# A list scheduler's picture of waits, products of constants in TensorE's gaps, and chunk values copied out by two engines, in a two-layer RWKV-7 and latent-attention trunk

## The chip, the cores and the metric

The kernel runs on one NeuronCore of a Trainium2 chip. Its five instruction streams are TensorE (PE; its weight loads are shown apart as PEld), VectorE (DVE), ScalarE (ACT), GpSimd (POOL) and SyncE (SP), which starts the DMAs. The metric is the device time of one execution in microseconds (us); the smaller is the better.

## The reference, cut to what matters

The input is a sequence of 512 positions with 16 learned ones put ahead, so T = 528, of width 1024. Layer 0 projects it (w_in, 2048 wide per kind) to v, k, r and a gate g and to two small products for decay and a, and then runs a recurrence over time, independently for 32 heads of 64 channels:

```python
def step(S, inp):
    r_t, w_t, k_t, v_t, a_t, b_t = inp
    sa = jnp.einsum('bhij,bhj->bhi', S, a_t)
    S = S * w_t[:, :, None, :] + sa[..., None] * b_t[:, :, None, :] + v_t[..., None] * k_t[:, :, None, :]
    return S, jnp.einsum('bhij,bhj->bhi', S, r_t)
```

The result is normalised per head, gated and projected by w_out. Layer 1 is a causal attention with 16 heads over low-rank keys and values, gated and projected again. All is float32 at the interface.

## The kernel before

Layer 0 keeps channels on partitions and time on the free axis. Two heads share a tile (a pair p = 0 to 15; head 0 on partitions 0 to 63, head 1 on 64 to 127). The recurrence is done in chunks: chunk 0 holds the 16 learned positions, chunks 1 to 8 hold 64 positions each. For a pair, `products` and `inverse` make the triangular matrices of all nine chunks (many small products, half of them float16), and `chunk(p, ci)` then runs the nine steps one after the other. A step goes: two products into PSUM (`ALR` by `SV`), VectorE copies them to `xs`, two products (`xs` by `Qf`), ScalarE copies the two halves into `SV`, two products (`SV` by `KBt`), VectorE scales and adds the two halves into `SV` of the next chunk with `sd`, which GpSimd made ready. The next chunk waits for that. Chunks 1 to 7 are run by `recur`, which takes its PSUM from the pool `pc` of one bank; chunks 0 and 8 are run by `ends` and take it from the pool `pw` of four banks. That is 7 x 16 = 112 steps on `pc` and 32 on `pw`.

Between these steps TensorE does the projections of k, r and g (`gemm`, `multiply`): each output is 48 products of 128x264, two PSUM banks at a time. A number is split into a high and a low float32r part, so every product is done three times (high by high, high by low, low by high). Layer 1 works in the same way with larger products.

Nothing of this order is written by hand. Every part is a generator (a stage) that yields steps; `Flow.note` records the instructions of a step in place of issuing them, and `Flow.run` is a list scheduler. For each stage's first open step `Flow.start` works out when each of its operations could begin: when its engine is free (`self.free`), when its inputs are ready plus a lag from engine to engine (`LAGS`), and when the PSUM bank it touches was last used by another engine (`self.access`). The operation with the earliest start is issued, and `Flow.issue` moves the picture on by the operation's cost (`Flow.cost`). The line that chooses is

```python
if s[1][j].wide and self.hungry(t):
    t -= self.AHEAD
if best is None or t < best[0] - (self.SLACK if i > best[1] else -self.SLACK):
    best = (t, i, j)
```

Stages stand in order of rank: finish, recur, ends, sides, invert, within, prepare and so on, the layer-1 stages, the weights' loads and splits, and the large products (`gemm`, `gating`) last. With SLACK at zero the earlier start wins whatever the rank. `wide` marks an operation of TensorE with 256 columns or more; where the scheduler's own count of columns says that TensorE is short of work (`hungry`), a wide product is taken 0.25 us early. The engines carry out what they are given in that order, each waiting for its semaphores; a picture that is wrong about a wait costs time on the engine that reaches the waiting instruction. All instructions are issued by one line (293 before the change, 306 after), so the trace's groups are told apart by the names of their tiles.

## Time and profile before

| what | value |
|---|---|
| median of 3 runs | 1622.15 us (1618.94 to 1629.05) |
| the profiled execution's own time | 1630.59 us |
| its span, from the first to the last instruction | 1628.6 us |
| mean granted TensorE clock, as a share of 2.4 GHz | 0.954 |
| busy TensorE / VectorE / ScalarE / GpSimd | 92% / 62% / 59% / 50% of the span |
| TensorE products (and as many weight loads) | 13788 |

A stretch is named by its start and end in us from the span's start. Layer 0's recurrence runs from about 246 to 960 us, its last large products to 1107, layer 1 behind that. A busy time counts an instruction from its start to its end; products of TensorE overlap, so 100% busy is not its peak. The granted clock is 1.00 (2.4 GHz) or 0.50 (1.2 GHz) at any one moment.

### The profile page before, as it was taken

The numbers are of one execution on the slowest core, as the hardware profiler recorded it, in microseconds if no ns is written. First come the engines' busy times: TensorE is split into PE (matmuls) and PEld (weight loads), VectorE is DVE, ScalarE is ACT, GpSimd is POOL, SyncE is SP. The second block draws the span as 40 slices with busy tenths as digits, with TensorE's granted clock in tenths as the row PEclk, the third lists the DMA queues.
The fourth block names the chain that finished last, engine by engine and source line by source line (L and its number), as shares of the span: only waits on it lengthen the run. The fifth ranks groups of instructions, "written<-read, shape, count | busy, mean of one in ns | idle before, by whom it ended". The sixth has DMA issues, their size and how long they took to land. (4 is left out here: it accounts for less than half of the span.)

```text
span 1628.6 us, 36087 instructions
## 1 busy us (share of the span) xinstructions
PE 1498.6 (92%) x13788; PEld 1292.3 (79%) x13788; DVE 1006.9 (62%) x2144; ACT 967.1 (59%) x2451; POOL 806.3 (50%) x1039
## 2 busy tenths in 40 slices
PE   4889889999999999998899999999989999999997
PEld 3889878777877877777787889998778888877786
DVE  7994677788778678777664542035366666666503
ACT  3557657876767677775686865445454544544532
POOL 5353566566556465554565565745522222332554
PEclk8999999999989899998897999999989999999999
DMA  3446522122112121121402247532211111111332
GB/s 112 143 173 230 188 85 87 41 68 74 68 58 71 42 77 65 61 81 55 167 35 73 86 139 256 159 110 92 68 52 40 56 46 52 59 56 43 110 93 82
DMA packets 84700, 148.66 MB, mean 91 GB/s; under 512 B 9392, under 2 KB 18480, under 8 KB 84528
## 3 DMA queue, kind: packets, MB, share of 16 engines
q1 hardware_dynamic: 84528, 146.37, 27.7%
q8 instruction: 108, 1.77, 0.4%
q14 instruction: 64, 0.52, 0.1%
HBM read 112.87 MB, written 33.46 MB: 90 GB/s over the span
## 5 line engine op out<-in xcount | busy, mean ns | idle before, releaser
L293 POOL TENSOR_TENSOR w<-wraw,w 128x512 fp32r<-128x512 f32 (+1 forms) x278 | 358.7, 1296 | 431.3 <-ACT w L293 393.5
L293 PE MATMUL pg<-x,w 128*128 128x264 f32 x2256 | 401.7, 310 | 5.3 <-ACT k L293 3.9
L293 PEld LDWEIGHTS pg<-x,w 128*128 128x128 f32 x2256 | 313.1, 196 | 21.1 <-ACT k L293 4.9
L293 ACT ACTIVATE w<-wraw 128x512 fp32r<-128x512 f32 (+1 forms) x278 | 169.6, 616 | 154.1 <-DMA wraw<-wo 51.0
L293 POOL TENSOR_TENSOR sd<-SV,PC 64x64 f32<-64x64 f32 x224 | 80.7, 360 | 73.8 <-DVE SV L293 63.9
L293 PE MATMUL pb<-u,w 128*128 128x512 f32 x384 | 106.4, 410 | 5.3 <-DVE sg L293 5.3
L293 PE MATMUL pg<-lat,w 128*128 128x512 f32 (+1 forms) x480 | 109.4, 370 | 0.0
L293 DVE SCALAR_TENSOR_TENSOR SV<-pc,PC,sd 64x64 f32<-64x64 f32 x224 | 63.2, 282 | 55.3 <-PE pc L293 49.0
L293 PEld LDWEIGHTS pg<-lat,w 128*128 128x128 f32 x480 | 82.2, 201 | 10.6
L293 PEld LDWEIGHTS pb<-u,w 128*128 128x128 f32 x384 | 71.4, 196 | 19.6 <-DVE sg L293 6.0
L293 PE MATMUL pg<-O,w 128*128 128x512 f32 x336 | 81.7, 401 | 1.8 <-DVE O L293 1.2
L293 ACT ACTIVATE SV<-pc 64x64 f32<-64x64 f32 x224 | 48.4, 216 | 49.5 <-PE pc L293 41.0
L293 PEld LDWEIGHTS pg<-O,w 128*128 128x128 f32 x336 | 63.8, 192 | 17.1 <-DVE O L293 2.0
L293 PEld LDWEIGHTS <-Mb 128*128 128x128 f16 x1152 | 51.9, 98 | 20.8 <-issue 4.5
L293 DVE TENSOR_TENSOR Xs<-pw,masks 128x128 f16<-128x128 f32 (+1 forms) x160 | 48.0, 305 | 30.5 <-PE pw L293 18.6
L293 POOL TENSOR_TENSOR Lb<-Qf,Mh 64x256 f16<-64x256 f32 (+1 forms) x64 | 50.7, 793 | 28.4 <-ACT Mh L293 23.9
L293 DVE SCALAR_TENSOR_TENSOR sg<-sg,par,rs 128x264 f32<-128x264 f32 x32 | 15.6, 518 | 73.5 <-ACT rs L293 73.5
L293 ACT ACTIVATE Qb<-pw 128x256 f16<-128x256 f32 (+1 forms) x128 | 51.8, 410 | 15.3 <-PE pw L293 13.7
L293 PE MATMUL pw<-Tm,Mb 128*128 128x32 f16 (+1 forms) x864 | 55.8, 183 | 4.9 <-DVE Tm L293 4.2
L293 ACT ACTIVATE PT<-py 128x128 fp32r<-128x128 f32 (+1 forms) x64 | 27.9, 436 | 53.6 <-PE py L293 53.6
L293 ACT ACTIVATE Tm<-pw 128x128 f16<-128x128 f32 (+1 forms) x160 | 44.9, 288 | 24.2 <-PE pw L293 22.0
L293 DVE TENSOR_TENSOR sg<-sg,rs 128x256 f32<-128x256 f32 x12 | 7.1, 596 | 72.8 <-ACT rs L293 72.8
(396 smaller groups left out, 3857.6 us busy)
## 6 DMA issues: line engine op xcount, KB each, us to landing
wraw<-wr SPq DMA_DIRECT2D x120, 256.0 KB, 2.7
wraw<-wo SPq DMA_DIRECT2D x64, 256.0 KB, 2.7
wraw<-wi SPq DMA_DIRECT2D x46, 256.0 KB, 2.6
d_v<-gx SPq DMA_DIRECT2D x16, 264.0 KB, 2.1
d_c<-o SPq DMA_DIRECT2D x16, 264.0 KB, 2.2
d_a<-vx SPq DMA_DIRECT2D x16, 264.0 KB, 2.8
c<-d_c SPq DMA_DIRECT2D x16, 264.0 KB, 2.9
a<-d_a SPq DMA_DIRECT2D x16, 264.0 KB, 3.3
```

The source lines that it names most:

```text
L293: getattr(eng, method)(*args, **kw)
```

## The change

The order is made anew for the whole program by another picture:

- SLACK goes from 0 to 0.12 us: an operation of a stage of lower rank is taken only if it can start more than 0.12 us earlier.
- An engine that writes at another start partition than in its instruction before starts later by TAIL (0.10 to 0.13 us); VectorE's operations with two inputs in SBUF wait while GpSimd is in an operation; the lags from ScalarE and VectorE to TensorE fall from 0.23 and 0.22 to 0.19 and 0.17 us; `wide` is kept for float32r alone.
- `cold`: while layer 0 runs, where the earliest start on any engine is GAP (0.15 us) or more behind the end of TensorE's last operation in the picture, and the columns counted for the time before are under FED, a product of two constant tiles (`masks`, float16, 128x256) is issued to TensorE. Its result is not read. It goes to columns 256 to 511 of the PSUM bank whose first columns `recur` uses; that bank is now one fixed tile (`self.bank`) in place of a new tile of `pc` for each product.
- In `chunk` the first half of the new `SV` is copied out by ScalarE as before, the second by VectorE.

```diff
-    SLACK = 0.0
+    SLACK, DEFER = 0.12, 0.0
     AHEAD, SPARE = 0.25, 0.35
+    GAP, FED = 0.15, 3400
...
+            op.wide = eng == "tensor" and ins[0].dtype == F32R and cost[0][2] >= 256
+            if eng in self.TAIL:
+                op.part = out.offset // out.ap[0][0]
+                op.shares = eng == "vector" and sum(x.space != PSUM and len(x.shape) > 1 and x.shape[-1] > 1 for x in ins) > 1
...
-    LAGS = {("tensor", "scalar"): 0.2, ("tensor", "vector"): 0.2, ("scalar", "tensor"): 0.23, ("vector", "tensor"): 0.22,
+
+    TAIL = {"vector": 0.11, "scalar": 0.13, "gpsimd": 0.1}
+
+    LAGS = {("tensor", "scalar"): 0.2, ("tensor", "vector"): 0.2, ("scalar", "tensor"): 0.19, ("vector", "tensor"): 0.17,
...
+        elif op.eng in self.TAIL and op.part != self.part.get(op.eng, 0):
+            t += self.TAIL[op.eng]
...
+            if op.shares and self.port[0] < t < self.port[1]:
+                t = self.port[1]
+            if op.eng == "gpsimd":
+                self.port = t, t + op.cost
+            self.part[op.eng] = op.part
             t += op.cost
...
+    def cold(self, now):
+
+        t = self.free["tensor"]
+        if now < t + self.GAP:
+            return False
+        while self.past and self.past[0][0] < t - self.TICK:
+            self.past.pop(0)
+        if sum(c for _, c in self.past) >= self.FED:
+            return False
+        out, w, x = self.warm
+        op = Op("tensor", ("matmul", (out, w, x), dict(start=True, stop=True)), [(x.shape[1] / 2.4e3, 0.025, x.shape[1])], set(), set(), set(), set())
+        self.issue([op], 0, t + 0.03)
+        return True
...
+            if self.warm and self.cold(best[0]):
+                continue
...
+        self.bank = self.psum("pc", 512, 1)
+        self.flow.cut[self.bank.tensor.name] = 256
+        self.flow.warm = self.bank[:, 256:512], m[:, 0:128], m[:, 128:384]
...
-        for hs, h in heads:
-            nc.scalar.activation(SV[hs, ci, h, :], x[hs], AF.Copy)
+        nc.scalar.activation(SV[H0, ci, 0, :], x[H0], AF.Copy)
+        nc.vector.tensor_copy(SV[H1, ci, 1, :], x[H1])
...
-            small = lambda: self.psum("pc", 512, 1)
+            small = lambda: self.bank
```

What each engine is given differs in few counts: TensorE gets 246 products of `masks` (and their weight loads) more, ScalarE loses 144 copies of 64x64 (112 from `pc`, 32 from `pw`), VectorE gains as many. All else is the same work in another order, on every engine.

The first place is TensorE at the last but one chunk of the first pair, where chunk 7 begins. `pc` is the chunk bank, `py` the chunks' outputs, `o`, `Qb`, `Mb` belong to the inversion for the next pairs; a name in square brackets is the semaphore of an engine that the instruction waits for. Before:

```order
L293 LDWEIGHTS o_2360
L293 MATMUL pw_4035<-Qb,o_2360 128x64
L293 LDWEIGHTS o_2360
L293 MATMUL pw_4035<-Qb,o_2360 128x64
L293 LDWEIGHTS o_2360
L293 MATMUL pw_4035<-Qb,o_2360 128x64
L293 MATMUL pc_4041<-SV_2606,ALR_2518 64x64 [waits DVE_49]
L293 MATMUL pc_4041<-SV_2606,ALR_2518 64x64
L293 MATMUL py_3851<-ALR_2518,SV_2606 64x64 x2
L293 MATMUL pw_4024<-SV_3063,KBt_3064 64x64 [waits Activation_49] x2
```

and after the change:

```order
L306 LDWEIGHTS o_2553
L306 MATMUL pw_3929<-Qb,o_2553 128x64
L306 LDWEIGHTS masks
L306 MATMUL pc_353<-masks 128x256 [waits DVE_49]
L306 LDWEIGHTS masks
L306 MATMUL pc_353<-masks 128x256 [waits DVE_49]
L306 LDWEIGHTS masks
L306 MATMUL pc_353<-masks 128x256
L306 MATMUL py_3808<-MR_2711,SV_2708 64x64 x2
L306 MATMUL pc_353<-SV_2708,ALR_2680 64x64 x2
L306 MATMUL py_3808<-ALR_2680,SV_2708 64x64 x2
L306 MATMUL pw_3943<-SV_3199,ALR_3031 64x64 x2
```

Three products of constants now stand between the inversion's products and the chunk's next step; the first two wait for VectorE, and the chunk's own product behind them no longer carries that wait. Over the whole order the 246 products stand in 117 runs; in 54 runs one or more of them wait for VectorE or ScalarE (63 waits), and 88 of the products stand at or behind the last wait of their run. 54 of the readers of the chunk bank (43 of VectorE, 11 of ScalarE) stand behind a product of constants that was issued after the product they read.

The second place is VectorE in chunk 3 of the first pair, from the copy to `xs` to the two halves of the next chunk's `SV`. Before:

```order
L293 COPY xs_3645<-pc_3646 128x64 [waits PE_49]
L293 TENSOR_TENSOR Xs<-pw_3653,masks 128x160 [waits DVE_49,PE_49,Activation_49]
L293 TENSOR_TENSOR ALR_3450<-r_3182,P_3333 128x8x64
L293 SCALAR_TENSOR_TENSOR r_3182<-r_3182,par,sq_3404 128x528 [waits DMAHW7_49,DVE_49,Pool_49]
L293 SCALAR_TENSOR_TENSOR SV_2606<-pc_3704,PC_2493,sd_3647 64x64 [waits PE_49]
L293 SCALAR_TENSOR_TENSOR SV_2606<-pc_3704,PC_2493,sd_3647 64x64
L293 TENSOR_TENSOR Xs<-pw_3714,masks 128x128 [waits PE_49,Activation_49]
L293 TENSOR_TENSOR Qf_3708<-pw_3709,masks 64x256 [waits PE_49]
```

and after the change:

```order
L306 COPY xs_3623<-pc_353 128x64 [waits PE_49]
L306 SCALAR_TENSOR_TENSOR inv_3323<-k_2790,par,inv_3323 128x528
L306 TENSOR_TENSOR Qb<-Mb,masks 64x5x64 [waits DVE_49]
L306 COPY SV_2708<-pc_353 64x64 [waits Activation_49,Pool_49]
L306 TENSOR_TENSOR Xs<-pw_3666,masks 128x128 [waits DVE_49,PE_49]
L306 TENSOR_TENSOR Tm_2590<-pw_3668,masks 128x320 [waits PE_49]
L306 SCALAR_TENSOR_TENSOR SV_2708<-pc_353,PC_2670,sd_3624 64x64 [waits PE_49]
L306 SCALAR_TENSOR_TENSOR SV_2708<-pc_353,PC_2670,sd_3624 64x64
```

VectorE now also copies a half of `SV` out of `pc` between the two, and that copy waits for ScalarE (which copies the other half out of the same bank) and for GpSimd.

## Rows read from the trace of the kernel before

**Rows 1.** The page of the profile: its span, and the granted TensorE clock by slice.

```profile
span 1628.6 us, 36087 instructions
...
PEclk8999999999989899998897999999989999999999
```

**Rows 2.** Busy time by stretch: length, engines, clock, DMA share and GB/s.

```profile
246.00:960.00 714.00, 678.24 (x8434) 559.71 (x8432) 510.80 (x1298) 512.14 (x1459) 410.88 (x685) 0.95 0.22 72
...
1107.00:1560.00 453.00, 422.88 (x2370) 360.21 (x2369) 257.86 (x531) 225.22 (x509) 159.06 (x134) 0.96 0.20 62
...
0.00:246.00 246.00, 197.70 (x1583) 186.19 (x1584) 186.56 (x236) 139.86 (x307) 119.53 (x125) 0.94 0.46 156
```

**Rows 3.** The same view, the time just ahead of four falls of the clock.

```profile
450.20:453.60 3.40, 2.56 (x42) 2.10 (x44) 3.23 (x7) 2.01 (x6) 2.39 (x6) 0.99 0.03 7
521.80:525.20 3.40, 1.89 (x26) 1.45 (x27) 3.34 (x8) 2.91 (x11) 1.74 (x6) 1.00 0.21 80
743.80:747.20 3.40, 1.99 (x31) 1.63 (x28) 3.24 (x6) 0.71 (x3) 2.19 (x6) 0.98 0.24 82
866.50:870.00 3.50, 2.50 (x36) 2.01 (x36) 2.58 (x8) 2.83 (x8) 2.23 (x4) 1.00 0.16 56
```

**Rows 4.** Timeline of TensorE ahead of 870 us: start, length, what [idle before].

```profile
866.77 0.34 PE L293 MATMUL py<-MR,SV 128*64 128x64 f32 x4
867.98 0.34 PE L293 MATMUL pc<-SV,ALR 128*64 128x64 f32 x4 [0.88 <-DVE SV L293]
```

**Rows 5.** Busy time by stretch, the six stretches at half clock.

```profile
453.60:463.80 10.20, 9.99 (x83) 7.99 (x80) 6.69 (x22) 4.88 (x14) 3.00 (x6) 0.50 0.34 110
525.30:542.20 16.90, 16.90 (x151) 13.98 (x151) 10.25 (x21) 9.34 (x29) 8.79 (x15) 0.50 0.05 16
747.20:760.70 13.50, 13.33 (x114) 10.95 (x113) 7.02 (x17) 6.59 (x20) 4.38 (x9) 0.50 0.06 19
788.10:794.80 6.70, 6.70 (x55) 5.66 (x54) 5.14 (x11) 3.71 (x11) 6.12 (x16) 0.50 1.01 345
808.60:815.30 6.70, 6.70 (x64) 5.78 (x62) 3.03 (x10) 5.92 (x14) 1.92 (x3) 0.50 0.51 164
870.00:893.80 23.80, 23.80 (x229) 19.70 (x230) 5.66 (x18) 15.71 (x48) 8.43 (x13) 0.50 0.15 46
```

**Rows 6.** Groups of TensorE, 246 to 960 us: count | busy us, mean ns | idle before.

```profile
L293 PE MATMUL pc<-SV,KBt 128*64 128x64 f32 x448 | 39.1, 255 | 7.4 <-ACT SV L293 7.1
...
L293 PE MATMUL pc<-xs,Qf 64*64 64x64 f32 x448 | 38.7, 252 | 5.4 <-DVE xs L293 5.3
...
L293 PE MATMUL pc<-SV,ALR 128*64 128x64 f32 x448 | 37.3, 247 | 6.6 <-DVE SV L293 6.5
...
L293 PE MATMUL pw<-masks,Mb 128*128 128x64 f16 x279 | 18.9, 195 | 1.5 <-ACT Mb L293 0.8 <-DVE Qb L293 0.5
```

**Rows 7.** The same view for ScalarE and VectorE, 246 to 960 us.

```profile
L293 ACT ACTIVATE SV<-pc 64x64 f32<-64x64 f32 x224 | 48.4, 216 | 49.5 <-PE pc L293 41.0 <-POOL sd L293 2.0 <-PE pw L293 1.3
...
L293 DVE SCALAR_TENSOR_TENSOR SV<-pc,PC,sd 64x64 f32<-64x64 f32 x224 | 63.2, 282 | 55.3 <-PE pc L293 49.0 <-POOL ALR L293 1.1
...
L293 DVE COPY xs<-pc 128x64 f32<-128x64 f32 x112 | 24.7, 220 | 24.5 <-PE pc L293 23.1
```

**Rows 8.** Timeline of one chunk: start us, length us, engine, what.

```profile
306.08 0.23 DVE L293 COPY xs<-pc 128x64 f32<-128x64 f32 x1
...
306.36 0.27 PE L293 MATMUL pc<-xs,Qf 64*64 64x64 f32 x2
...
307.36 0.45 ACT L293 ACTIVATE SV<-pc 64x64 f32<-64x64 f32 x2
...
308.59 0.60 DVE L293 SCALAR_TENSOR_TENSOR SV<-pc,PC,sd 64x64 f32<-64x64 f32 x2 [2.29 <-PE pc L293]
```

**Rows 9.** The chain that ended last: start us, length us, what.

```profile
1535.98 67.31 PE pg L293 x291
```

More of the change, by code (lines that the diff above doesn't have):

```diff
@@ L150, in __init__ @@
         self.used, self.access = {}, {}
-        self.fill, self.columns = 0.0, {}
+        self.fill, self.columns, self.past, self.warm = 0.0, {}, [], None
         Places.prior.clear()
@@ L154, in __init__ @@
         self.waiting, self.done = [], False
+        self.part, self.port = {}, (0.0, 0.0)
         self.cut = {}
@@ L184, in note @@
         else:
-            self.step.append(Op(eng, call, cost, outs, set(names), {x.tensor.name for x in ins if x.space == PSUM}, banks))
+            op = Op(eng, call, cost, outs, set(names), {x.tensor.name for x in ins if x.space == PSUM}, banks)
+            op.wide = eng == "tensor" and ins[0].dtype == F32R and cost[0][2] >= 256
+            if eng in self.TAIL:
+                op.part = out.offset // out.ap[0][0]
+                op.shares = eng == "vector" and sum(x.space != PSUM and len(x.shape) > 1 and x.shape[-1] > 1 for x in ins) > 1
+            self.step.append(op)
     def later(self, stage):
@@ L306, in issue @@
                 self.columns[j] = self.columns.get(j, 0) + cols * (1 - part)
+                self.past.append((self.fill, cols))
                 t += 0.0025
         else:
+            if op.shares and self.port[0] < t < self.port[1]:
[3 more added lines that the diff above has]
+            self.part[op.eng] = op.part
             t += op.cost
@@ L363, in run @@
                         continue
-                    if s[1][j].wide and self.hungry(t):
-                        t -= self.AHEAD
+                    if s[1][j].wide:
+                        t += -self.AHEAD if self.hungry(t) else 0.0 if "finished" in self.events else self.DEFER
                     if best is None or t < best[0] - (self.SLACK if i > best[1] else -self.SLACK):
@@ L383, in __init__ @@
         self.events, self.closes = [], []
-        self.wide = eng == "tensor" and cost[0][2] >= 256
+        self.part, self.shares = 0, False
+        self.wide = False
 def bc(m, n):
@@ L455, in tables @@
             yield
+        m = self.masks.rearrange("p m t -> p (m t)")
+        self.bank = self.psum("pc", 512, 1)
+        self.flow.cut[self.bank.tensor.name] = 256
+        self.flow.warm = self.bank[:, 256:512], m[:, 0:128], m[:, 128:384]
     def norm(self):
@@ L1468, in gemm @@
             yield from self.out_o(j, outs[j])
+        flow.warm = None
         g.single.close()
+        g.banks["pc"] = g.pool("pc", 1, PSUM)
         g.wide = ExitStack()
@@ L2039, in build @@
         g.consts()
-        g.banks = {n: g.pool(n, b, PSUM) for n, b in (("pg", 2), ("pc", 1), ("py", 1))}
+        g.banks = {n: g.pool(n, b, PSUM) for n, b in (("pg", 2), ("py", 1))}
         g.single = ctx.enter_context(ExitStack())
-        g.banks["pw"] = g.pool("pw", 4, PSUM, ctx=g.single)
+        for n, b in (("pw", 4), ("pc", 1)):
+            g.banks[n] = g.pool(n, b, PSUM, ctx=g.single)
         g.xkp = g.pool("xkp", 1)
```

## The prediction

> **What bounds the kernel now.** I read the page first: a span of 1628.6 us, and a granted clock that is nine or ten tenths in most slices and eight in some [rows 1]. TensorE is busy nearly everywhere, so the second view is its busy time by stretch. In layer 0's recurrence, 246 to 960 us, it is busy 678.2 of 714.0 us with 8434 products, while VectorE is busy 510.8 and ScalarE 512.1 [rows 2]. Products of the projections are always in stock there to fill TensorE, so what this stretch loses is the time in which TensorE stands still (714.0 - 678.2 = 35.8 us) and the time in which its clock is halved.
>
> The third view shows how the clock falls. In the 3.4 us ahead of four falls TensorE was busy 2.56, 1.89, 1.99 and 2.50 us only, with the clock still granted whole; VectorE was busy 3.23, 3.34, 3.24 and 2.58 us [rows 3]. The timeline ahead of the last of them shows what TensorE stood for: 0.88 us in front of a chunk's first product, until VectorE had written SV [rows 4]. So one late chunk step costs its own wait and then a stretch at half clock. There are six such stretches in the recurrence, 10.2 + 16.9 + 13.5 + 6.7 + 6.7 + 23.8 = 77.8 us at a clock of 0.50, in which TensorE is busy 77.4 us [rows 5]: it doesn't wait there, it is slow.
>
> What they cost is bounded from both sides. They hold 83 + 151 + 114 + 55 + 64 + 229 = 696 products [rows 5]; the other 636.2 us hold 8434 - 696 = 7738 [rows 2, 5], or 12.16 a us, at which 696 would need 57.2 us: a loss of 20.6 us. If TensorE's work alone set the pace, half of the time would be lost, 38.9 us. As it is busy all the time there, I take the middle, 30 us. The fourth view, TensorE's groups, says which instructions it stood still for: the three kinds of chunk products on pc had 7.4, 5.4 and 6.6 us of idle time before them, 19.4 us together [rows 6].
>
> **The change, part by part.** All terms are made against the profiled execution's own 1630.59 us (its span and 2.0 us around it); the median of the runs is 1622.15, so the sum's difference is taken off that, as 8.4 us of profiling belong to neither kernel.
>
> *The products of constants.* Nothing in the trace is that product, so I bound it. The dense end of layer 1 does 291 products of 512 columns in 67.31 us, 0.231 us each [rows 9]; half the columns is 0.116 us, say 0.12 with its start (an estimate from that row). 246 of them are 29.5 us. If all fall into time in which TensorE stands still anyway they cost nothing, which 35.8 us of idle time would allow; if none does, 29.5 us. The order decides between the ends: 88 of them stand at or behind the last wait of their run. What they wait for is a reader of the chunk bank, and that is what the chunk's next step waits for too, so these 88 run when the chunk could go on: 88 x 0.12 = 10.6 us. The other 158 stand ahead of a wait, and the wait hides them. Take +10.6 (0 to 29.5).
>
> That they wait at all is a matter of the bank. In the kernel before every chunk product and its reader on VectorE share one bank and follow each other with a gap of some 0.05 us (a copy to xs from 306.08 for 0.23, the next product at 306.36) [rows 8]; the new products go to other columns of the same bank, and the order shows 63 of them waiting for a reader. The Trainium skill, PSUM — Partial Sum Buffer, section "PSUM bank collisions raise a hardware error", says that a TensorE write and another engine's read of the same bank and partitions must be kept apart even at disjoint columns. By columns alone the 10.6 us would be nothing; by that rule they stand, and no run here shows it yet.
>
> *Readers behind a constant product.* 54 reads of the chunk bank now wait for a product of constants as well. A float16 product with 64 columns lasts 0.195 us from start to end [rows 6]; with 192 columns more at 0.231 / 512 a column [rows 9] it is 0.28 us. At worst 54 x 0.28 = 15.1 us; nothing where the reader's engine was still at something else, which is why the scheduler saw a gap. Take a quarter, +4 (0 to 15.1).
>
> *Two engines for SV.* ScalarE's two copies last 0.216 us each, 0.45 us as a pair [rows 7, 8]. Now ScalarE's copy is followed by a semaphore and VectorE's: the copy to xs lasts 0.220 us [rows 7], the step from one engine to another some 0.05 us [rows 8], so 0.22 + 0.05 + 0.22 = 0.49 us. So the copies are not side by side, as the order shows VectorE's copy waiting for ScalarE's. The step is 0.04 us longer, 144 times: 6 us if every one is waited for. ScalarE is rid of 144 x 0.216 = 31.1 us, and VectorE gets 144 x 0.22 = 31.7 us, 4% of 714. Most chunk steps are covered by projection products (19.4 us of idle time over 112 steps of three products [rows 6] is little). Take +2 (-10 to +32, the upper end if VectorE is what the chunks wait for throughout).
>
> *Another picture.* The scheduler prices a 64x64 copy from PSUM on ScalarE at 0.05 + 64 x 0.00083 = 0.10 us and VectorE's scaled sum at 0.07 + 0.055 + 64 x 0.00106 = 0.19 us; the trace has 0.216 and 0.282 [rows 7]. Both come in pairs, one on each half of the partitions, so the picture of before was 0.2 to 0.4 us early at each chunk, and TensorE reached the chunk's product too early and waited. TAIL adds 0.13 and 0.11 to such an operation, which makes 0.23 and 0.30: near the trace. SLACK takes the chunks ahead of the fill by up to 0.12 us. The most that this can win is the 35.8 us of idle time [rows 2]; if the new picture is as wrong in the other direction, it loses the chunk products' 19.4 us once more [rows 6]. I take two thirds of the 19.4 us as won: -13.
>
> *The clock.* Fewer chunk waits, and constant products in those that are left, take away the short idle spells ahead of the falls [rows 3]. I take three quarters of the 30 us as given back: -22 (0 to -38.9). A stretch that has once begun has no gaps for the constants to fill, so one late step that the picture misses still costs a whole one.
>
> *The rest.* In 0 to 246 and 1107 to 1560 us TensorE stands still for 48.3 and 30.1 us [rows 2]. The order changes there too, and no products are put in (from layer 1's first outputs on). I see no reason for either sign: 0 (-10 to +10, a third of the 30.1).
>
> Sum: +10.6 + 4 + 2 - 13 - 22 + 0 = -18.4 us, 1612.2 for a profiled execution and 1622.15 - 18.4 = 1603.8 us for the median, 1.1% faster.
>
> **The rivals.** *VectorE is the bound of the chunk, and the change loads it.* For: ahead of three of the four falls VectorE was busy 3.2 to 3.3 of 3.4 us, and TensorE waited for its SV [rows 3, 4]; 144 copies are added just there. Against: over the whole stretch it is busy 72% [rows 2]. If half of the added 31.7 us comes onto the chunks, and the chunks stay as late as they were, so that the clock falls as before and the picture wins nothing: 15.9 + 10.6 = 26.5, so 1648 us. It decides from where the copies cost more than the 20 us that the other terms win (13 + 22 - 10.6 - 4). *No change.* The clock gives back half of what I take (-11), the constants and readers cost 14.6, the order wins nothing, two engines 2: +5.6, so 1628 us. For it: the constants only move the wait, and TensorE is as late as before. *A larger gain.* The picture is right throughout: the clock gives back all 30, the order 27 of the idle time, against 10.6 + 2: -44, so 1578 us. For it: all falls looked at begin with the same kind of late step [rows 3]. Against: VectorE's load.
>
> **How the numbers follow.** About 1% is what a measurement of this kernel can tell from no change. Forecast 0.46, with its own range 1590 to 1616 (the order's term from -20 to -5, the constants' from 5 to 18), of which about two thirds lie below 1606: 0.31 faster and 0.15 the same. Larger gain 0.19, faster. No change 0.18, the same. VectorE 0.17, slower. So faster 0.50, same 0.33, slower 0.17. The range that should hold 8 in 10 goes from 1577, just under the larger gain's time (some two fifths of that case lie below), to 1638, which leaves out a little more than half of the slower case.
>
> **What would show it.** Right: between 246 and 960 us fewer than 30 us at a clock of 0.50, idle time in front of the chunk products well under 19.4 us, the constants' group with 246 products and little idle time ahead of them, VectorE's copy of SV starting just behind ScalarE's. Wrong: stretches at half clock as long as before, or chunk products that wait for VectorE's SV for more than 19.4 us, or a recurrence that ends later than 960 us by more than the projection products moved into it (3138 products with weights stand ahead of the last chunk's product of xs by Qf in the new order, 2922 in the old; 216 x 0.12 = 26 us). The forecast falls if layer 1 or the first 246 us move by over 10 us.

## The result, and the profile after

The change is slower: 1685.55 us (median of 4 runs, 1676.25 to 1692.89) against 1620.55 for the kernel before beside it, a ratio of 1.0393 with an interval of 1.0323 to 1.0464. The forecast was 1604 us; the time lies above the range's end of 1638. The profiled execution took 1676.25 us, 45.7 more than the 1630.59 of before; that is less than the 64.9 us between the medians, as the profile of before is of an execution slower than all its timed runs (1615.05 to 1629.05) and that of the change is of its fastest.

The page of the profile after, its span and granted clock by slice, as [rows 1]:

```profile
span 1674.5 us, 36575 instructions
...
PEclk8999879897999868877899999999999999999999
```

The clock is worse in most of slices 5 to 20 (167 to 837 us), nearly all of them in the recurrence, and better behind it. Busy time by stretch, as [rows 2] (length, PE, PEld, DVE, ACT and POOL with their counts, granted clock, DMA share, GB/s):

```profile
0.00:246.00 246.00, 197.95 (x1613) 188.23 (x1615) 186.80 (x232) 142.20 (x308) 124.52 (x127) 0.92 0.48 157
246.00:960.00 714.00, 663.11 (x7889) 536.69 (x7886) 497.53 (x1321) 427.91 (x1187) 362.97 (x629) 0.89 0.20 63
...
1107.00:1560.00 453.00, 429.97 (x2606) 371.28 (x2605) 253.20 (x532) 225.35 (x517) 167.34 (x144) 0.99 0.22 67
```

Between 246 and 960 us TensorE does 7889 products where it did 8434, though 226 of the 7889 are products of constants. It is busy 15 us less, at a clock of 0.89 in place of 0.95. The half-clock stretches that begin behind 246 us, as [rows 5], are now thirteen up to the recurrence's end, 157.1 us in all; the three longest are

```profile
602.60:636.80 34.20, 30.76 (x285) 21.95 (x285) 20.05 (x60) 13.70 (x41) 10.01 (x23) 0.50 0.12 40
776.70:800.60 23.90, 20.61 (x148) 13.58 (x147) 11.39 (x37) 4.19 (x12) 5.06 (x11) 0.50 0.13 44
377.40:394.40 17.00, 15.27 (x142) 11.55 (x140) 9.40 (x26) 9.72 (x30) 5.69 (x11) 0.50 0.07 19
```

In [rows 5] TensorE was busy for 77.4 of 77.8 us at half clock; here it is busy for 142.3 of the 157.1, so it is slow and waits too. TensorE's groups in this stretch, as [rows 6], with the new products first:

```profile
L306 PE MATMUL pc<-masks 128*128 128x256 f16 x226 | 57.3, 327 | 14.9 <-DVE SV L306 10.3 <-ACT SV L306 2.5 <-DVE xs L306 1.4
L306 PE MATMUL pc<-SV,KBt 128*64 128x64 f32 x392 | 35.8, 265 | 8.3 <-DVE SV L306 8.0
L306 PE MATMUL pc<-xs,Qf 64*64 64x64 f32 x392 | 34.7, 258 | 0.5 <-DVE xs L306 0.2
L306 PE MATMUL pc<-SV,ALR 128*64 128x64 f32 x392 | 33.3, 253 | 3.8 <-DVE SV L306 3.6
```

Ahead of the chunk products stand 12.6 us of idle time, where [rows 6] had 19.4. But in these 714 us only 98 of the 112 chunk steps are done (392 products of 448): the last sum into SV starts at 957.2 us before and at 1050.3 now. With all 112 steps, from 246 to 1060 us, it is 17.4 us:

```profile
L306 PE MATMUL pc<-SV,KBt 128*64 128x64 f32 x448 | 40.5, 263 | 12.0 <-DVE SV L306 11.6
L306 PE MATMUL pc<-xs,Qf 64*64 64x64 f32 x448 | 39.2, 256 | 0.5 <-DVE xs L306 0.2
L306 PE MATMUL pc<-SV,ALR 128*64 128x64 f32 x448 | 38.0, 251 | 4.9 <-DVE SV L306 4.7
```

Another 14.9 us stand ahead of the constants, which wait for the same readers, so the idle time went from 19.4 to 32.3 us; it did not fall. These 13 us more are still not the 93.

Where those 93 us are, the instructions' starts tell. For each of the 112 steps I took the time from its first product to the end of its second sum (the steps), and from there to the next step's first product; of these, those over 2.5 us (the long waits) stand apart. Before, the steps are 508 us, the short waits 78, the long ones 113 (12 of them). After, 491, 53 and 247 (23). So the chunks with their short waits run 42 us faster, and the recurrence stands still for 134 us more. All the long waits of these two kernels stand at two places: between two pairs, and ahead of a pair's fourth chunk, where `recur` waits for the second lane of the inversion. One of them, seen by the chunk bank's instructions from 754 to 780 us:

```profile
L306 PE MATMUL pc<-SV,ALR x4: 315/342/369, 777.3 to 777.5; 128*64 128x64 f32 x4
...
L306 DVE SCALAR_TENSOR_TENSOR SV<-pc,PC,sd x2: 278/284/291, 757.2 to 757.5; 64x64 f32<-64x64 f32 x2
```

SV is ready at 757.8, the next chunk begins at 777.3. TensorE isn't idle for that: its row of busy time for the wait has 15.85 of 19.20 us,

```profile
758.00:777.20 19.20, 15.85 (x238) 13.72 (x236) 13.94 (x25) 15.12 (x44) 10.82 (x19) 0.99 0.23 75
```

most of it projections (6.6 us) and the inversion. The timeline shows what had to come first, the last steps of that inversion (`Mb`, `Q`, `Qf`):

```profile
773.75 0.77 DVE L306 SCALAR_TENSOR_TENSOR r<-r,par,sq 128x528 f32<-128x528 f32 x1 [1.15 <-POOL ALR L306]
...
774.55 0.64 ACT L306 ACTIVATE P<-r 128x528 fp32r<-128x528 f32 x1 [0.78 <-DVE r L306]
...
775.22 0.91 ACT L306 ACTIVATE Mb<-Tm 64x320 f16<-64x320 f16 x2
...
775.74 0.32 PE L306 MATMUL pw<-masks,Mb 128*128 128x64 f16 x5 [0.95 <-ACT Mb L306]
...
776.10 0.44 ACT L306 ACTIVATE Q<-pw 128x320 f16<-128x320 f32 x1
...
776.59 0.33 PE L306 MATMUL pw<-Q,Qb 128*128 128x64 f16 x5 [0.53 <-ACT Q L306]
...
777.03 0.49 DVE L306 SCALAR_TENSOR_TENSOR Qf<-pw,Q 128x320 f32<-128x320 f32 x1
777.35 0.48 PE L306 MATMUL pc<-SV,ALR 128*64 128x64 f32 x4
```

VectorE stands for 1.15 us at another pair's `r`, ScalarE for 0.78 us at its `P`, and the inversion's `Mb` is behind that `P`; TensorE in turn waits 0.95 us for `Mb`. The engines take their instructions in the order given, so in this wait the order holds up what the recurrence needs.

What a recurrence that stands still costs the kernel can be read from TensorE's line on the page, before and then after:

```profile
PE 1498.6 (92%) x13788; PEld 1292.3 (79%) x13788; DVE 1006.9 (62%) x2144; ACT 967.1 (59%) x2451; POOL 806.3 (50%) x1039
PE 1534.5 (92%) x14034; PEld 1306.8 (78%) x14034; DVE 1037.7 (62%) x2288; ACT 930.6 (56%) x2307; POOL 805.4 (48%) x1039
```

Of the 45.9 us between the spans TensorE is busy for 35.9, with the 246 constants and the lower clock in it, and idle for 10.0. The 93 us don't appear as idle time, as other products fill most of them.

### The profile page after: what moved, and what is told of

Its sections match the earlier page's. It is cut to its first block, busy times and chain, and to the rows that moved or that the text cites. A ratio compares the mean times of both kernels' runs of the same rounds, so it can differ in the third digit from the quotient of the medians.

```text
span 1674.5 us, 36575 instructions
## 1 busy us (share of the span) xinstructions
PE 1534.5 (92%) x14034; PEld 1306.8 (78%) x14034; DVE 1037.7 (62%) x2288; ACT 930.6 (56%) x2307; POOL 805.4 (48%) x1039
## 4 chain that ended last, share of the span: by engine, by line
PE 60%; DVE 10%; ACT 6%; issue 3%; POOL 2%; DMA 1%; SPq 0%; DVEq 0%; ACTq 0%; POOLq 0%
PE pg L306 27%; PE pw L306 11%; PE pc L306 8%; PE py L306 5%; PE pb L306 4%; PE pd L306 2%; PE ps L306 2%; DVE qr L306 2%; DVE SV L306 2%; DVE sg L306 1%; PE pe L306 1%; DVE P L306 1%; POOL w L306 1%; ACT w L306 1%; DVE Y L306 1%
## 5 line engine op out<-in xcount | busy, mean ns | idle before, releaser
L306 POOL TENSOR_TENSOR w<-wraw,w 128x512 fp32r<-128x512 f32 (+1 forms) x278 | 366.6, 1324 | 397.2 <-ACT w L306 340.8
L306 PE MATMUL pg<-x,w 128*128 128x264 f32 x2304 | 386.4, 303 | 2.8 <-DMA x<-d_xg 2.0
L306 POOL TENSOR_TENSOR sd<-SV,PC 64x64 f32<-64x64 f32 x224 | 75.7, 338 | 126.1 <-DVE SV L306 117.0
L306 PE MATMUL pb<-u,w 128*128 128x512 f32 x384 | 103.0, 402 | 5.0 <-DVE sg L306 5.0
L306 PE MATMUL pg<-lat,w 128*128 128x512 f32 (+1 forms) x480 | 105.6, 363 | 0.2 <-DVE q L306 0.2
L306 PE MATMUL pc<-masks 128*128 128x256 f16 x246 | 61.7, 327 | 14.9 <-DVE SV L306 10.3
L306 PE MATMUL pw<-ALR,KB 64*128 64x128 f32 (+1 forms) x576 | 59.0, 349 | 1.7 <-DVE Qb L306 1.3
L306 DVE COPY SV<-pc 64x64 f32<-64x64 f32 x112 | 25.5, 228 | 55.2 <-ACT SV L306 40.9
L306 DVE TENSOR_TENSOR Xs<-pw,masks 128x128 f16<-128x128 f32 (+1 forms) x160 | 47.2, 305 | 19.0 <-PE pw L306 10.6
```

The costliest lines, as they stand in the source:

```text
L306: getattr(eng, method)(*args, **kw)
```

## The experiments

Eighteen kernels, each beside the kernel before on the same chip. None leaves out a part of the reference's computation. "Clock" and "products" are TensorE's from 246 to 960 us, steps and long waits as above, "copies" the time between the two copies of SV, summed over the 112 steps. The columns behind the ratio are from one profiled execution each.

| kernel | us | ratio (interval) | clock | products | steps | long waits | copies |
|---|---|---|---|---|---|---|---|
| before | 1620 | 1 | 0.95 | 8434 | 508 | 113 | 4 |
| the change | 1685.55 | 1.0393 (1.0323 to 1.0464) | 0.89 | 7889 | 491 | 247 | 40 |
| k_noprod | 1673.71 | 1.0329 (1.0282 to 1.0377) | 0.83 | 7689 | 484 | 257 | 36 |
| k_act | 1687.79 | 1.0431 (1.0380 to 1.0482) | 0.89 | 7820 | 500 | 246 | 54 |
| k_both | 1669.57 | 1.0310 (1.0264 to 1.0355) | 0.85 | 7737 | 483 | 256 | 50 |
| r_picture | 1679.33 | 1.0377 (1.0334 to 1.0421) | 0.85 | 7673 | 528 | 204 | 78 |
| p_slack0 | 1723.13 | 1.0653 (1.0618 to 1.0689) | 0.79 | 7486 | 620 | 94 | 67 |
| p_notail | 1668.86 | 1.0312 (1.0276 to 1.0348) | 0.87 | 7922 | 434 | 266 | 5 |
| p_rest | 1647.93 | 1.0178 (1.0144 to 1.0211) | 0.89 | 8081 | 479 | 165 | 7 |
| b_slack | 1641.22 | 1.0134 (1.0101 to 1.0168) | 0.91 | 8191 | 458 | 228 | 3 |
| b_tail | 1717.23 | 1.0609 (1.0581 to 1.0637) | 0.82 | 7479 | 661 | 74 | 89 |
| b_tailtime | 1699.79 | 1.0504 (1.0476 to 1.0531) | 0.85 | 7653 | 503 | 182 | 3 |
| b_tail_sv | 1731.94 | 1.0707 (1.0671 to 1.0744) | 0.86 | 7436 | 728 | 28 | 120 |
| b_tail_rest | 1702.82 | 1.0507 (1.0470 to 1.0545) | 0.83 | 7584 | 568 | 146 | 3 |
| b_slackrank | 1789.29 | 1.1058 (1.1026 to 1.1090) | 0.81 | 6818 | 778 | 44 | 19 |
| b_lags | 1643.95 | 1.0170 (1.0135 to 1.0205) | 0.94 | 8234 | 475 | 174 | 3 |
| b_lagsup | 1667.98 | 1.0244 (1.0179 to 1.0310) | 0.89 | 8039 | 510 | 150 | 3 |
| b_exact | 1697.23 | 1.0464 (1.0423 to 1.0504) | 0.84 | 7644 | 480 | 216 | 4 |
| b_eps | 1621.28 | 1.0023 (0.9996 to 1.0050) | 0.96 | 8495 | 501 | 113 | 3 |
| b_const | 1633.16 | 1.0080 (1.0049 to 1.0112) | 0.93 | 8363 | 512 | 123 | 6 |

**Which part of the change.** Three kernels keep the changed order word for word; r_picture has the new picture alone, with both copies on ScalarE and no constants, and the order that the scheduler makes of that.

```diff
 k_noprod (and k_both), in cold:
+        op.calls = []
         self.issue([op], 0, t + 0.03)
 k_act (and k_both), planned for VectorE but issued on ScalarE (the lines that do so left out):
-        nc.vector.tensor_copy(SV[H1, ci, 1, :], x[H1])
+        nc.vector.copy_on_scalar(SV[H1, ci, 1, :], x[H1])
 r_picture, in run and in chunk:
-            if self.warm and self.cold(best[0]):
-                continue
-        nc.vector.tensor_copy(SV[H1, ci, 1, :], x[H1])
+        nc.scalar.activation(SV[H1, ci, 1, :], x[H1], AF.Copy)
```

> The changed kernel in the very order that it has, with the 246 products of constants left out of TensorE's stream (the scheduler still counts them, so nothing else moves). Theory C (the constants and their waits on the chunk bank are the loss): 1655 us or less, chunk steps shorter by 0.3 us or more. Theory V (the copy on VectorE behind ScalarE's) and theory P (the order that the new picture makes): within 10 us of the changed kernel's 1685; if the constants hold the clock, slower than it, with more time at half clock than its 167 us between 246 and 1050 us.

> The changed kernel in the very order that it has, but the second half of SV is copied out by ScalarE, at the place where VectorE's copy stood in the order. Theory V: the gap between the two copies falls from a mean of 0.36 us to under 0.1, the 112 chunk steps win some 35 us, 1655 us or less. Theories C and P: the gap falls but the time stays within 12 us of 1685, since the chunks wait for something else next.

> Both of these at once, still in the changed kernel's order: no constants, both copies on ScalarE. What is left is the order by the new picture (made for other instructions). Theory P: 1660 us or more. Theories C and V together: 1640 us or less.

> The new picture alone: no products of constants, both copies on ScalarE, and the order made anew for that, so that the picture fits what is issued. Theory P: 1650 us or more, the recurrence still ends later than 1000 us. Theories C and V: 1630 us or less, near the kernel before or faster than it.

The new picture alone is 61 us slower than before (1679.33 - 1617.88), nearly the whole of it. Ahead of its chunk products, from 246 to 1060 us, TensorE is idle for 25.3 us, more than the 19.4 of before:

```profile
L306 PE MATMUL pc<-SV,KBt 128*64 128x64 f32 x448 | 42.2, 273 | 11.2 <-ACT SV L306 11.0
L306 PE MATMUL pc<-xs,Qf 64*64 64x64 f32 x448 | 41.6, 269 | 8.5 <-DVE xs L306 8.1
L306 PE MATMUL pc<-SV,ALR 128*64 128x64 f32 x448 | 39.4, 259 | 5.6 <-DVE SV L306 5.4
```

Over the whole run it does the same 13788 products as before; of the 55.2 us by which the span is longer it is busy for 24.7, at a mean clock of 0.915 in place of 0.954, and idle for 30.5:

```profile
PE 1523.3 (90%) x13788; PEld 1312.4 (78%) x13788; DVE 997.9 (59%) x2144; ACT 961.7 (57%) x2451; POOL 810.0 (48%) x1039
```

The second copy's engine makes no difference clear of the noise (k_act against the change, k_both against k_noprod: the intervals overlap). The time between the copies, which k_act should have closed, did not fall (54 us, 40 in the change), so k_act tests the engine alone; p_notail and b_tailtime below have whole pairs and are slow all the same. Without the constants the kernel is 0.6% faster in one pair (1.0393 - 1.0329, some 10 us, the intervals overlap) and 18 us in the other (k_act - k_both, the intervals are apart). It was expected to be slower without them if they hold the clock; they do hold it, and it is not. The stretch 246 to 960 us of k_noprod, against the change's row above:

```profile
246.00:960.00 714.00, 662.64 (x7689) 552.70 (x7688) 500.66 (x1325) 429.29 (x1190) 365.29 (x629) 0.83 0.20 63
```

With the constants the clock is 0.89 in place of 0.83, but TensorE's busy time is the same, 663.1 and 662.6, and it does no more of the other products: 7889 - 226 = 7663 against 7689. The Trainium skill, TensorE: Matmul & The Clock Gate, section "Terms", puts the price of throttled time at that time by the share of the clock that is missing; by it 0.06 of 714 us is an estimated 43 us. The 226 constants held TensorE for 46 us, counted in the trace from each one's start to the next product's start or its own end, so by the page they come out about even; the runs have a net cost of 10 and 18 us. The time at half clock doesn't decide alone: k_noprod has 317 us of it in the whole run, the change 220, and k_noprod is no slower.

b_const was to have the constants on before's picture, with the fixed bank that they need.

```diff
+            if self.warm and self.cold(best[0]):
+                continue
...
-            small = lambda: self.psum("pc", 512, 1)
+            small = lambda: self.bank
```

> The kernel before with the products of constants alone, on before's picture of waits, and the fixed bank that they need. Theory 'the order': the picture is what made the kernel slower, and the products cost about what they did in the changed order (12 to 18 us, against a clock that they raise): 1615 to 1640, with a granted clock above before's 0.954. Rival 'the products too': they push chunk products and inversions apart in any order, 1650 or more.

0.8% slower, 15 us by the medians. But the run hardly tests the constants. On before's picture the scheduler found room for only 13 of them:

```profile
L294 PE MATMUL pc<-masks 128*128 128x256 f16 x13 | 4.0, 352 | 2.3 <-DVE SV L294 1.6 <-ACT SV L294 0.4 <-DVE xs L294 0.3
```

They are busy for 4.0 us, so most of the loss must lie elsewhere, in the fixed bank or in the order, which is another one from some 457 us on. The clock of the whole run isn't above before's, as was expected: 0.952 in the median, 0.964 for before beside it. What 246 constants would do in before's order isn't shown by any run.

**Which part of the picture.**

```diff
 b_slack, on before:
-    SLACK = 0.0
+    SLACK = 0.12
 b_tail, on before (with part and its bookkeeping as in the change):
+        elif op.eng in self.TAIL and op.part != self.part.get(op.eng, 0):
+            t += self.TAIL[op.eng]
 b_lags, on before:
-    ("scalar", "tensor"): 0.23, ("vector", "tensor"): 0.22
+    ("scalar", "tensor"): 0.19, ("vector", "tensor"): 0.17
 p_slack0, p_notail, p_rest, on r_picture: SLACK 0; TAIL 0; both
```

> The kernel before with SLACK 0.12 in place of 0 and nothing else. Theory S (rank ahead of an earlier start by up to 0.12 us is what spoils the order, since TensorE and the others then wait for chunk steps in place of filling): 1650 us or more. Theory T (TAIL spoils it: the second of a chunk's two copies or sums now looks 0.11 to 0.13 us later than any other waiting operation of that engine, so that one is put between the two): within 12 us of the kernel before, 1618.

> The kernel before with TAIL alone (0.11, 0.13 and 0.10 us at a change of the start partition). Theory T: 1650 us or more, and a mean gap between ScalarE's two copies of SV of 0.3 us or more, where the kernel before has 0.04. Theory S: within 12 us of 1618.

> The picture-only kernel (1679 us; no constants, both copies on ScalarE) with TAIL at zero, SLACK, lags and the rest as in the change. Theory T: 1640 us or less, gap between the two copies under 0.1 us (0.70 with TAIL). Theory S: 1660 us or more.

> The picture-only kernel with SLACK at 0 and TAIL kept. Theory S: 1640 us or less. Theory T: 1665 us or more, as rank can then hold nothing together at all.

> The new picture alone with TAIL and SLACK both at nothing: what is left of it are the lags 0.19 and 0.17, the rule for the port that VectorE and GpSimd share, wide for long float32r products only, and the fixed bank. If the parts add up (this picture without TAIL 1669, SLACK alone +22): about 1647. Rival 'SLACK and the rest make each other worse': 1620 to 1630, nothing is left. Rival 'the rest is what costs': 1665 or more, SLACK gives nothing here.

> The kernel before with the two shorter lags alone (ScalarE to TensorE 0.19, VectorE to TensorE 0.17, before 0.23 and 0.22). Theory 'the lags are the rest': this picture without TAIL and without SLACK's 22 us is some 28 us over before, and TensorE's instructions that wait for a copy look ready 0.04 to 0.05 us sooner than they are; then 1640 to 1655. Rival 'the port, the wide products or the bank': 1612 to 1628, no difference from before.

Each part alone is slower: TAIL by 98 us, SLACK by 22 (between what its two theories expected), the shorter lags by 26. SLACK and the lags add up: SLACK costs 1.3% alone and as much on the rest without TAIL (p_rest to p_notail). With TAIL it doesn't: there SLACK wins 2.8% back (p_slack0 to r_picture). The port's rule, `wide` and the fixed bank leave no net cost beside the lags (p_rest 1.0178, b_lags 1.0170).

The table shows two ways to lose. With TAIL and no SLACK the steps are long (620 and 661 us) and the long waits short. With SLACK the steps are short (458 and 434), as the recurrence is taken ahead of the inversion, and it then stands still for twice as long (228 and 266). The change is of the second kind.

**Does TAIL cost by parting the pairs?** In b_tail's order other instructions of ScalarE stand between the two copies of 58 of the 112 steps; in before's, of one. I took that for the cause. b_tailtime counts TAIL when an instruction is put down, and not when the next one is chosen.

```diff
-        elif op.eng in self.TAIL and op.part != self.part.get(op.eng, 0):
+        elif tail and op.eng in self.TAIL and op.part != self.part.get(op.eng, 0):
...
-            self.issue(stages[i][1], j, self.start(stages[i][1], j))
+            self.issue(stages[i][1], j, self.start(stages[i][1], j, True))
```

> The kernel before, with TAIL's 0.11, 0.13 and 0.10 us counted in the clock of the engine (when an instruction is put down) but not in the choice of the next one. Theory 'the choice': TAIL's 98 us come from the second half of a pair looking later than another stage's instruction, which is then put between the halves; with the halves side by side again the time is near before's, 1605 to 1640, and the gap between the two copies of a chunk stays under 0.1 us. Rival 'the times': the prices with TAIL are a worse forecast of when engines come free, whoever is chosen; then the time stays above 1680.

The pairs are whole again (copies 3 us, steps 503) and the kernel is still 82 us slower: my theory falls. The time came back as long waits, 182 us. Then I divided TAIL by what an instruction writes, and turned the stages' rank round under SLACK.

```diff
 b_tail_sv (b_tail_rest: "SV" not in):
-                op.part = out.offset // out.ap[0][0]
+                op.part = out.offset // out.ap[0][0] if "SV" in out.tensor.name else 0
 b_slackrank, with SLACK 0.12:
-[self.finish(), self.recur(), self.ends(8), self.ends(0), self.sides(), self.invert(0), self.invert(1), self.within(), self.prepare(),
+[self.finish(), self.sides(), self.invert(0), self.invert(1), self.within(), self.prepare(), self.recur(), self.ends(8), self.ends(0),
```

> The kernel before with TAIL counted only for instructions that write SV (the chunks' copies and sums). Theory 'the inversion is late': TAIL costs by making the half-partition instructions of the inversion look late, so that the halves of a pair are ready later than the recurrence; TAIL on SV alone then costs little, 1615 to 1650, though the copies of SV are pulled apart. Rival 'the chunk itself': most of the 98 us are here, 1680 or more, with the gap between a chunk's two copies over 0.5 us in the mean.

> The kernel before with TAIL counted for all instructions but those that write SV. Theory 'the inversion is late': most of TAIL's 98 us, 1680 to 1710, with the recurrence standing still for longer ahead of its fourth chunk and between pairs (113 us in waits of over 2.5 us before). Rival 'the chunk itself': 1615 to 1650.

> The kernel before with SLACK 0.12, and the stages' rank turned round: the inversion and what prepares it stand ahead of the recurrence. SLACK alone cost 22 us with the recurrence first: its chunks went faster and then waited for the inversion (waits of over 2.5 us: 228 us, before 113). Theory 'the inversion is late': with the inversion first these waits shrink under 150 us and the time is 1610 to 1630, under SLACK alone. Rival 'the chunk is late': chunks that come second to the inversion are slower by more than that, 1650 or more.

The two parts of TAIL don't add up to its 98 us either: on SV alone it costs 113 us, by longer steps (728), and on all the rest 84 us, by longer waits and steps. ScalarE's timeline in b_tail_sv shows the first kind:

```profile
627.15 0.22 ACT L301 ACTIVATE SV<-pc 64x64 f32<-64x64 f32 x1
627.45 0.84 ACT L301 ACTIVATE Mb<-Tm 64x256 f16<-64x256 f16 x2
628.32 0.22 ACT L301 ACTIVATE SV<-pc 64x64 f32<-64x64 f32 x1
```

The inversion's two `Mb` stand between the halves, for 0.95 us that the chunk waits. The reverse is no better: with the inversion ahead of the recurrence the long waits shrink to 44 us, as the theory said, and the steps grow to 778, so that "the chunk is late" holds for b_slackrank and the kernel is 170 us slower. Its stretch has the fewest products of all:

```profile
246.00:960.00 714.00, 598.94 (x6818) 501.28 (x6815) 415.31 (x1072) 406.95 (x1174) 317.62 (x551) 0.81 0.17 56
```

So there are two chains, the chunks and the inversion that they wait for, and in these runs an order that serves either at the other's cost loses.

**Luck, direction, dearer prices.**

```diff
 b_eps, on before (b_lagsup: 0.27 and 0.27):
-    ("scalar", "tensor"): 0.23, ("vector", "tensor"): 0.22
+    ("scalar", "tensor"): 0.231, ("vector", "tensor"): 0.221
 b_exact, on before:
-            return 0.07 + 0.055 * point + n * (0.52e-3 if fast else 1.06e-3)
+            return 0.155 + 0.055 * point + n * (0.52e-3 if fast else 1.06e-3)
-            return (0.05 if ins[0].space == PSUM else 0.095) + 0.08 * point + n * 0.83e-3
+            return (0.165 if ins[0].space == PSUM else 0.21) + 0.08 * point + n * 0.83e-3
-    ("scalar", "tensor"): 0.23, ("vector", "tensor"): 0.22
+    ("scalar", "tensor"): 0.115, ("vector", "tensor"): 0.135
...
```

> The kernel before with both lags 0.001 us longer: the order is the same up to some 70 us into the recurrence and then another one, by ties that fall the other way. Theory 'prices decide': a picture that is the same to 0.001 us makes an equally good order, 1610 to 1626. Rival 'the order of before is a lucky one': any other costs what the lags cost, 1635 to 1650.

> The kernel before with the lags to TensorE 0.27 us both, in place of 0.23 and 0.22 (the lags of the change are 0.19 and 0.17, and cost 26 us alone). Theory 'counted twice': hand-overs that look later than they are cost as those of TAIL do, though less (0.04 to 0.05 us a step in place of 0.11 and 0.13): 1630 to 1665. Rival 'longer is better': the shorter lags cost since the picture was too early, and longer ones win, 1612 or less.

> The kernel before with 0.115 us more in every price of ScalarE and 0.085 in every price of VectorE (as the trace has them), and as much less in the lags behind these engines, so that an instruction alone hands on its result when it did before. Theory 'counted twice': TAIL costs because it adds to the two chains a delay that the lags held already; a picture with the same hand-over and the right prices then costs little or nothing, 1600 to 1640. Rival 'dearer prices': whatever makes VectorE and ScalarE look busier lets TensorE take the projections ahead of the chains, as with TAIL: 1680 or more.

In the traces the orders of before and of b_eps part at some 460 us, 200 us into the recurrence and not 70; behind that b_eps has another order, and it has the time of before. With b_const's 0.8% these are two more orders by before's picture, and neither costs what the lags cost. So the order of before isn't a single lucky one, as far as two neighbours tell. Lags that are 0.04 and 0.05 us shorter cost 26 us, as much longer 47 us (1667.98, just above the 1630 to 1665 of its theory). b_exact keeps the hand-over and makes both engines' instructions dearer; "counted twice" falls, as it is 76 us slower. Its prices are the instructions' durations, and by the last section those are too dear where an instruction begins before the one ahead of it has ended, so it tests dearer prices, not exact ones. The waits for SV from 246 to 1055 us (total, times, longest us), in before and then in b_exact:

```profile
DVE SV L293 <- PE pc L293: 49.0, 39, 3.3
...
ACT SV L293 <- PE pc L293: 41.0, 40, 3.3
```

```profile
DVE SV L293 <- PE pc L293: 80.0, 64, 3.9
...
ACT SV L293 <- PE pc L293: 67.2, 65, 6.8
```

Both engines reach the chunk's instruction and stand there for TensorE's product 57 us longer in sum, with all their other work, the inversion's too, queued behind it; the long waits rise to 216 us. No kernel beat the one before. The constants' neighbour, the two engines on before's picture, wasn't tried.

## Why the prediction was wrong

**Another picture: -13.** This is the step that failed: alone it is +61 (r_picture, with the clock's fall in it), far outside its own bounds (-35.8 to +19.4). The step went from "prices nearer the trace" to "less idle time ahead of the chunk products". That doesn't follow: this idle time rose, from 19.4 to 25.3 us in r_picture. And it was the wrong measure. The long waits rose by 91 us there and by 134 in the change; TensorE does other products in most of that time, so most of it appears in no idle row of [rows 6]. I had read what TensorE waits for and not how long the recurrence stands still, so neither bound held. The premise was too large as well: "0.2 to 0.4 us early" left out the lags that the picture counts behind a price. With 0.23 us of lag the picture of before has a pair of copies handed on after 2 x 0.10 + 0.23 = 0.43 us, and the trace after about 0.45 + 0.05 = 0.50 [rows 8]; it was under 0.1 us early. "SLACK takes the chunks ahead of the fill" was right, but it takes them ahead of the inversion too.

**The clock: -22.** Wrong sign: 157.1 us at half clock in place of 77.8. It was made to hang on fewer chunk waits, and these didn't come: r_picture, without constants, has a clock of 0.85.

**Constants and readers: +10.6 and +4.** The runs have 10 and 18 us, but with the clock's gain in it, which stood in another term; so the agreement is partly luck. From one constant's start to the next one's the trace has 0.109 us at full clock, as the 0.12 said, and 0.213 at half clock, where 105 of the 246 fell. They do wait for the chunk bank's readers (14.9 us ahead of them), as the order had shown.

**Two engines: +2.** Nothing in the runs speaks against it: no difference clear of the noise in the changed order. The hand-over is 0.10 us in the median of the 112, not 0.05; ScalarE's copy at 1048.85 lasts 0.22, VectorE's begins at 1049.17:

```profile
1048.85 0.22 ACT L306 ACTIVATE SV<-pc 64x64 f32<-64x64 f32 x1 [2.83 <-PE pc L306]
1049.17 0.23 DVE L306 COPY SV<-pc 64x64 f32<-64x64 f32 x1 [1.95 <-ACT SV L306]
```

**The rest: 0 (±10).** It gained. The last sum into SV is 93 us later and the kernel 45.7, so some 47 us came back. From that sum to the end, before and then after:

```profile
957.50:1628.60 671.10, 625.20 (x3800) 548.50 (x3799) 309.76 (x612) 316.60 (x689) 278.41 (x233) 0.97 0.28 88
1050.60:1674.50 623.90, 588.18 (x3577) 510.26 (x3575) 297.38 (x606) 297.22 (x653) 261.41 (x218) 0.99 0.28 85
```

Some 220 products fewer are left, as they were done in the recurrence (the trace has 231 projection products more there, where 216 were forecast: 28 us at 0.12 each), the clock is higher, and TensorE is idle for 35.7 us in place of 45.9.

**The rivals.** "VectorE is the bound" named the right side by a wrong mechanism: VectorE is busy for a smaller share of the recurrence than before (497.5 against 510.8 of 714 us), and k_act takes its copies away for nothing. Of the signs given in advance two came, half-clock stretches as long as before or longer and a recurrence that ends over 26 us late. The chunk products' own waits for VectorE's SV stay under 19.4 us (16.3). The forecast's own range goes by its terms to 1619 us, not 1616; nothing hangs on it. The 8.4 us put down to profiling are scatter: the change's profiled execution is its fastest run.

**Still open** is why dearer ScalarE and VectorE make such an order. Shown is that each part of TAIL, dearer prices and lags either way do, and where the recurrence then stands. Open too is how much of the loss comes by the waits themselves and how much by the clock that falls with them. That TensorE's own prices are too low (0.216 us for 512 columns, 0.231 in [rows 9]), so that the old low prices kept the three engines in step, was only argued.

## What to carry to other kernels

A list scheduler's prices are weights between chains as much as forecasts: try a truer picture part by part, and expect that one true correction alone may make the order worse. Where a recurrence is fed by another chain, measure how long it stands still and for what; a busy TensorE hides that. Compare waits over the same number of steps and not over the same microseconds. Products that only keep the clock up must win more than the time that they occupy; count them in the order before you read such a run.

## What the runs showed of the hardware

TAIL is real. In the kernel before ScalarE's timeline has pairs that change the half of the partitions, and pairs that don't; the group of `ysq` has the duration of one:

```profile
307.36 0.45 ACT L293 ACTIVATE SV<-pc 64x64 f32<-64x64 f32 x2
307.71 0.58 ACT L293 ACTIVATE SV<-pw 64x512 f32<-64x512 f32 x1
308.32 0.85 ACT L293 ACTIVATE ysq<-pw,eps_gn 128x264 f32<-128x264 f32 x2
```

```profile
L293 ACT ACTIVATE ysq<-pw,eps_gn 128x264 f32<-128x264 f32 x32 | 13.6, 475 | 0.9 <-PE pw L293 0.6
```

Two `ysq` on the same partitions take 0.85 us, 0.10 less than twice 0.475: the second begins before the first has ended. So does the copy at 307.71, 0.10 us before the pair's end at 307.81. The two SV copies, on different halves, take 0.45, 0.02 more than twice 0.216 [rows 7]. Set beside the program's order, the whole trace tells which instructions write at another start partition than the one ahead of them. Of those that follow within 0.06 us, the ones at the same start begin in the median 0.095 us before the end of the one ahead on ScalarE and 0.078 on VectorE (1156 and 1035 pairs), the ones at another start 0.024 and 0.031 us behind it (643 and 597). It is the start and not the number of partitions: two instructions of 64 partitions at the same start overlap by 0.094 and 0.080 (27 and 75 pairs). The differences, 0.12 and 0.11 us, are about TAIL's 0.13 and 0.11. The Trainium skill, ScalarE: Activation LUTs, section "What ACT_TABLE_LOAD costs", states an overlap of some 93 ns between activations; the trace agrees for the same start partition, and shows none across two. So the part of the new picture that the trace bears out was its dearest, as TAIL cost the most of the three.
